# A list scheduler gets other prices and priorities, and plans the norm's affine part behind the norm's tail

## The chip, the cores and the metric

The kernel runs on one core of one Trainium2 chip. The metric is the time of one execution on the device in microseconds (us), the median of several runs. A core has five engines that the program uses, each with its own fixed list of instructions: TensorE (PE, with PEld for its weight loads), VectorE (DVE), ScalarE (ACT), GpSimd (POOL) and SyncE (SP, which here only starts transfers). An instruction waits for the one before it on its engine, and for semaphores of other engines where it needs their results.

## What is computed

Two layers of an encoder trunk on x of 256 tokens by 1024 channels, in float32:

```python
for l in range(DEPTH):                       # DEPTH = 2
    h = hybrid_mixer(x, ...)                 # three mixers on x, gated and merged, then @ w_out
    x = layer_norm(DEEPNORM_ALPHA * x + h, ln1_g[l], ln1_b[l])
    f = conv_glu_ffn(x, ...)                 # (silu(conv(x @ w_gate)) * (x @ w_up)) @ w_down
    x = layer_norm(DEEPNORM_ALPHA * x + f, ln2_g[l], ln2_b[l])

def layer_norm(x, g, b):
    mu = mean(x); var = mean((x - mu) ** 2)
    return (x - mu) * rsqrt(var + LN_EPS) * g + b
```

The three mixers are a differential attention, a gated delta rule in both directions (its chunks need a triangular solve) and a windowed attention. So there are four norms: two in layer 0 and two in layer 1. The first three feed the next stage, and the last one writes the output.

## The kernel before

**Weights and products.** Nearly all of the time goes into products of x with weight blocks of 128x1024 floats, each streamed from memory once (`raw_take`, three buffers) in a fixed order. To reach float32 accuracy at the fast rate, a block is split into a high part (`hi_take`, a rounding copy on ACT) and a low part (`lo_take`, a subtraction on DVE), and x likewise into `xTh` and `xTl` (x is held with channels on the partitions for this). `mm3` then issues three matmuls for each product: high by high, low by high, high by low. A projection block (`mm_proj_ch`) is 8 x 3 = 24 matmuls of 256 columns. Some products are made with tokens on the partitions instead (`mm_token_major`, 512 columns); `mm_run` and `ch_run` are those of the output projections `wo` and `fd`, from `proj_tok`.

**The mixers' solve.** The triangular solve goes over seven levels. At each level matmuls (`ch_solve`) are followed by merges on DVE (COPY_PREDICATED into `h_solve`), each of which the next level's matmuls need. Four such chains run at once. Projection matmuls, weight splits, attention steps and convolution steps fill the gaps.

**The norm.** `proj_tok` makes the first token half complete, then calls `norm.tail(0)`, then runs the matmuls that were kept for the second half (the last go into `ch_run`), then calls `norm.tail(1)`. `part` adds the product to x and takes the statistics. `tail` aggregates them on DVE, adds epsilon, takes the power -1/2 on POOL (`s_tail<-s_tail,nhalf`, the pow), normalizes on DVE (`q_tail`, four instructions), transposes on PE (`ch_tail`, `at_tail`), scales on ACT or DVE (`e_tail`) and splits the result into `xTh` (a copy on ACT or a CAST on DVE) and `xTl` (a subtraction on DVE). Only `xTh` and `xTl` go on to the next products. `finish` makes the same normalized value in the other layout, for the residual sum much later: the affine part, eight POOL instructions for each of the first three norms, four `x<-q_tail,ya_ln_params` (times g) and four `x<-x,ya_ln_params` (plus b).

**What sets the order.** The kernel's code records its operations in a `Plan`. Each record gets a price (`_cost`), its data dependences, and a rank: the longest priced path to the end, plus `op.urgent`, plus an entry of the table `PRIO` for its label. `schedule` then plays a greedy list scheduler over the five engines: it takes the instruction that can start earliest by its prices and, where several can, that of the highest rank. Copies, scalings and affine steps recorded through `A` can go to ACT or DVE, and the scheduler picks one. It also doubles a matmul's price when the window before it was thin. At the end the operations are issued in the order of their planned starts, and this fixes each engine's list. `plan.hold(i, j)` makes the planner start i no sooner than j; it acts in the plan alone:

```python
    def hold(self, i, j):

        self.ops[i].known.add(j)
```

Semaphores are set from data dependences when the operations are issued. All instructions are issued from one line, which is why the profile shows L191 everywhere; after the change it is L194. Tile names tell what an instruction is.

Of the kernel before, what the change touches and what calls it, by code (L numbers as in the profile page):

```python
# [10 lines left out]
F32 = mybir.dt.float32  # L11
F32R = mybir.dt.float32r
# [3 lines left out]
ALU = mybir.AluOpType  # L16
# [3 lines left out]
P = 128  # L20
# [28 lines left out]
PRIO = {(1, 'a', 0): 2.3, (0, 'ckv', 0): -3.3, (0, 'gz', 8): 4.3, (1, 'wb', 7): -1.6, (0, 'k', 'ab', 0): 1.4, (1, 'cq', 0): 2.7, (0, 'gz', 9): -1.8, (1, 'k', 'q', 1): 8.1, (0, 'gz', 7): -2.0, (1, 'solve'): -4.6, (1, 'c', 'cq', 0): 2.5, (1, 'k', 'k', 1): -2.8, (0, 'aq', 1): -5.9, (0, 'gz', 3): 3.5, (0, 'ab', 0): -7.3, (0, 'gz', 10): 1.9, (0, 'c', 'ckv', 0): 1.8, (0, 'c', 0): -2.1, (0, 'k', 'gate', 1): 0.2, (0, 'q', 0): -7.1, (0, 'a', 2): 3.4, (1, 'v', 0): -4.1, (1, 'gz', 7): -1.0, (1, 'a', 'aq', 0): 4.5, (0, 'k', 0): -6.2, (0, 'q', 1): -7.6, (0, 'solve'): -2.7, (1, 'aq', 1): -4.7, (1, 'a', 'aq', 1): -1.4, (0, 'wb', 1): -0.6, (1, 'q', 1): 5.3, (0, 'gate', 0): 7.8, (0, 'a', 0): -0.7, (0, 'wb', 7): -1.0, (1, 'k', 'v', 0): -6.5, (1, 'wb', 2): 3.6, (0, 'a', 3): 2.0, (1, 'c', 0): 3.5, (1, 'k', 'v', 1): -5.3, (0, 'k', 'v', 1): -8.6, (1, 'c', 3): 3.4, (1, 'gate', 1): 5.4, (1, 'scan'): -1.6, (1, 'a', 2): 6.9, (1, 'av', 0): 5.6, (1, 'wb', 9): 2.5, (1, 'gz', 6): 1.6, (0, 'gz', 0): 1.3}  # L49
LOADS = (11, 12, 12)  # L50
PIECES = 2
PAIRS = ("s", "yc")
# [7 lines left out]
           "ACT": {"PE": 0.27, "ACT": 0.14, "DVE": 0.14, "POOL": 0.18, "SP": 1.42},  # L60
           "DVE": {"PE": 0.26, "ACT": 0.2, "DVE": 0.13, "POOL": 0.18, "SP": 1.22},
           "POOL": {"PE": 0.2, "ACT": 0.15, "DVE": 0.1, "POOL": 0.11, "SP": 0.2}}
DMA_ISSUE = 1.2
TICK = 10.24 / 3
FULL = 3060
ENGINES = ("PE", "ACT", "DVE", "POOL", "SP")
# [62 lines left out]


class _Op:
    __slots__ = ("eng", "call", "cost", "deps", "known", "outs", "lat", "tiles", "new", "rank", "table", "start", "end", "urgent", "ways", "succ", "left", "ready", "group", "banks", "load", "columns", "label")


class Plan:
# [43 lines left out]
    def record(self, *ways):  # L179
        op = _Op()  # L180
        op.ways = []
        for eng, name, fn, args, kw in ways:
            aps = [v for v in list(args) + list(kw.values()) if isinstance(v, bass.AP)]
            outs = [kw["out"] if "out" in kw else args[0]]
# [4 lines left out]
            ins = [ap for ap in aps if not any(ap is o for o in outs)]  # L189
            table = TABLES.get(next((v for v in args if isinstance(v, AF)), None)) if name == "activation" else None  # L190
            op.ways.append((eng, lambda fn=fn, args=args, kw=kw: fn(*args, **kw), _cost(eng, name, outs, ins, args, kw), table))  # L191
# [42 lines left out]
    def emit(self):  # L234
# [51 lines left out]
    def schedule(self, users, order):  # L286
# [13 lines left out]
        for i, op in enumerate(ops):  # L300
            if op.left == 0:
                for way in op.ways:
                    pending[way[0]].append(i)
        table, done, begun = None, 0, 0.0

        shared = {}

        def available(op, eng):
# [9 lines left out]
            for tag, names in need.items():  # L318
                k = queue[tag]
                if len(slots[tag]) < len(names) or not (self.tags[tag][1] or set(order[tag][k:k + len(names)]) == set(names)):  # L320
                    return None
                t = max(t, sorted(slots[tag])[len(names) - 1] + (DMA_ISSUE if op.eng == "SP" else 0.0))
            return t

        while done < len(ops):
            best, other = None, {}
            for e, todo in pending.items():
# [23 lines left out]
            s, e, i = best  # L351
            op = ops[i]
# [29 lines left out]
            for j in op.succ:  # L382
                n = ops[j]
# [98 lines left out]
def tile_encoder_trunk(ctx: ExitStack, tc: tile.TileContext, a: dict, out: bass.AP, depth=DEPTH, tap=None):  # L482
    nc = tc.nc
    plan = Plan()
# [3 lines left out]
    V, S, G, TE, SY = [plan.engine(*e) for e in (("DVE", nc.vector), ("ACT", nc.scalar), ("POOL", nc.gpsimd), ("PE", nc.tensor), ("SP", nc.sync))]  # L488
# [147 lines left out]
    ready = {}  # L636
# [98 lines left out]
    class Norm:  # L735
# [11 lines left out]
        def tail(self, tt):  # L747
# [11 lines left out]
            for c in range(2):  # L759
                xs = x[:, tt, c * 512:(c + 1) * 512]  # L760
# [4 lines left out]
                for q in range(2):  # L765
# [280 lines left out]
    def gdn(l, pr, ys):  # L1046
# [444 lines left out]
```

## Time and profile before

| | |
|---|---|
| median of 3 runs | 1016.73 us |
| the runs | 1016.73, 1015.3, 1017.36 us |
| the profiled execution | 1016.1 us |
| its span in the trace | 1014.4 us |
| PE busy | 977.3 us (96%), 7598 matmuls |
| DVE busy | 744.0 us (73%) |
| ACT busy | 578.1 us (57%) |
| POOL busy | 113.6 us (11%) |
| read from memory | 163.12 MB, 162 GB/s over the span |

The busy share is an average over stages. A row of the timeline gives the start, the length, the engine, the instruction with its tiles and shape, and how many equal ones in a row it stands for; in brackets is the idle time before it and what ended it. Matmuls are pipelined, so a matmul's shown length is longer than the step from one to the next.

### The profile page before, as it was taken

The page shows a single profiled execution, that of the slowest core. Times are in us where ns is not written, and L with a number is a line of the kernel's source. Part 1 is how long each engine was busy: PE and PEld are TensorE (multiplying, and loading weights), DVE is VectorE, ACT ScalarE, POOL GpSimd, SP SyncE. Part 2 cuts the span into 40 slices and gives each one's busy share as a digit, 9 for nine tenths or more (in the row PEclk, how much of TensorE's full clock was granted, in tenths as well). Part 3 has the DMA queues.
Part 4 walks back from the last instruction along what each step waited for, and adds up shares of the span by engine and source line. Part 5 has one row for each costly group of instructions (what it writes and reads, how often), then busy time and mean ns, then how long its engine had stood idle before and what let it go on. Part 6 is the DMA issues. An engine that isn't in the chain of part 4 may idle for free. (4 is left out here: it accounts for less than half of the span.)

```text
span 1014.4 us, 19166 instructions
## 1 busy us (share of the span) xinstructions
PE 977.3 (96%) x7598; PEld 909.8 (90%) x7598; DVE 744.0 (73%) x1324; ACT 578.1 (57%) x1026; POOL 113.6 (11%) x108
## 2 busy tenths in 40 slices
PE   7998999999998999999989999999999989999996
PEld 5897899998986999998869989999999779999885
DVE  6789886775589777665679998875657878667555
ACT  5665864785355565553535776766644536555432
POOL 0510002100005100000144200001000150000000
PEclk9999999999999999999999999999999999999998
DMA  7552434464573765665625444334546746555661
GB/s 233 188 169 82 127 100 146 162 202 121 184 219 114 225 205 185 184 186 185 211 84 162 146 133 141 93 112 128 178 136 198 231 145 201 181 188 184 192 192 67
DMA packets 50109, 165.43 MB, mean 163 GB/s; under 512 B 5751, under 2 KB 11271, under 8 KB 50020
## 3 DMA queue, kind: packets, MB, share of 16 engines
q1 hardware_dynamic: 48644, 159.78, 49.7%
q0 software_dynamic: 1376, 4.43, 1.6%
q8 instruction: 59, 0.97, 0.4%
q14 instruction: 30, 0.25, 0.1%
HBM read 163.12 MB, written 1.07 MB: 162 GB/s over the span
## 5 line engine op out<-in xcount | busy, mean ns | idle before, releaser
L191 PE MATMUL mm_proj_ch<-xTh,lo_take 128*128 128x256 f32 x1488 | 420.1, 285 | 2.2 <-DVE lo_take L191 2.2
L191 PE MATMUL mm_proj_ch<-xTh,hi_take 128*128 128x256 f32 x1488 | 420.1, 285 | 0.9 <-ACT hi_take L191 0.9
L191 PE MATMUL mm_proj_ch<-xTl,hi_take 128*128 128x256 f32 x1488 | 418.1, 284 | 2.0 <-DVE xTl L191 2.0
L191 DVE TENSOR_TENSOR lo_take<-raw_take,hi_take 128x1024 fp32r<-128x1024 f32 x219 | 271.3, 1244 | 117.2 <-ACT hi_take L191 106.4
L191 ACT ACTIVATE hi_take<-raw_take 128x1024 fp32r<-128x1024 f32 x213 | 225.5, 1059 | 226.4 <-PE mm_proj_ch L191 143.4
L191 PEld LDWEIGHTS mm_proj_ch<-xTh,lo_take 128*128 128x128 f32 x1488 | 279.7, 189 | 5.5 <-DVE lo_take L191 4.1
L191 PEld LDWEIGHTS mm_proj_ch<-xTl,hi_take 128*128 128x128 f32 x1488 | 279.2, 189 | 5.7 <-DVE xTl L191 3.4
L191 PEld LDWEIGHTS mm_proj_ch<-xTh,hi_take 128*128 128x128 f32 x1488 | 279.7, 189 | 2.6 <-ACT hi_take L191 1.6
L191 DVE TENSOR_TENSOR lo_proj_tok<-raw_proj_tok,hi_proj_tok 128x1024 fp32r<-128x1024 f32 x50 | 61.2, 1225 | 49.2 <-ACT hi_proj_tok L191 49.0
L191 ACT ACTIVATE hi_proj_tok<-raw_proj_tok 128x1024 fp32r<-128x1024 f32 x50 | 53.1, 1061 | 74.1 <-PE mm_run L191 33.8
L191 POOL TENSOR_TENSOR s_tail<-s_tail,nhalf 128x1 f32<-128x1 f32 x8 | 6.8, 855 | 367.8 <-DVE s_tail L191 367.8
L191 DVE SCALAR_TENSOR_TENSOR z_conv_silu<-mm_proj_ch,col_params,z_conv_silu 128x254 f32<-128x254 f32 (+1 forms) x96 | 39.6, 473 | 0.5 <-ACT z_conv_silu L191 0.4
L191 ACT ACTIVATE e_window<-e_window,s_window 128x256 f32<-128x256 f32 x57 | 27.2, 498 | 7.3 <-DVE s_window L191 7.2
L191 POOL DMA_DIRECT2D ya_ln_params<-in_lnp_dram x16 | 8.8, 554 | 188.3 <-PE mm_product L191 96.6
L191 DVE SCALAR_TENSOR_TENSOR g_product<-g_product,mm_product 128x512 f32<-128x512 f32 x24 | 16.3, 683 | 16.3 <-PE mm_product L191 16.2
L191 PE MATMUL mm_run<-hi_proj_tok,ile_encoder_trunk 128*128 128x512 f32 x88 | 27.3, 389 | 0.0
L191 PE MATMUL mm_run<-hi_proj_tok,tile_encoder_trunk 128*128 128x512 f32 x88 | 27.3, 389 | 0.0
L191 ACT ACTIVATE e_attention<-e_attention,s_attention 128x256 f32<-128x256 f32 x48 | 23.3, 500 | 5.6 <-DVE s_attention L191 5.6
L191 PEld LDWEIGHTS <-h_solve 128*128 128x128 f16 x448 | 20.7, 99 | 5.6 <-issue 2.8
L191 PE MATMUL mm_product<-yc_window,hi_take 128*128 128x256 f32 x128 | 24.0, 284 | 1.1 <-DVE yc_window L191 0.6
L191 PE MATMUL mm_product<-ya_attention,hi_take 128*128 128x256 f32 x128 | 24.4, 286 | 0.0
L191 POOL TENSOR_TENSOR x<-q_tail,ya_ln_params 128x512 f32<-128x512 f32 x12 | 22.2, 1865 | 11.2 <-DVE q_tail L191 11.2
(344 smaller groups left out, 1714.9 us busy)
## 6 DMA issues: line engine op xcount, KB each, us to landing
raw_take<-in_w_dram SPq DMA_DIRECT2D x226, 512.0 KB, 3.7
raw_proj_tok<-in_w_dram SPq DMA_DIRECT2D x60, 512.0 KB, 3.6
G_load_G<-band SPq DMA_DIRECT2D x24, 192.0 KB, 3.5
ya_ln_params<-in_lnp_dram POOLq DMA_DIRECT2D x16, 256.0 KB, 6.2
x<-in_xT_dram SPq DMA_DIRECT2D x4, 256.0 KB, 4.2
x<-in_x_dram SPq DMA_DIRECT2D x2, 512.0 KB, 4.5
out_dram<-x SPq DMA_DIRECT2D x8, 128.0 KB, 1.8
_tile_encoder_trunk<-in_w_dram SPq DMA_DIRECT2D x4, 128.0 KB, 3.7
```

The lines of the kernel that those rows point to most:

```text
L191: op.ways.append((eng, lambda fn=fn, args=args, kw=kw: fn(*args, **kw), _cost(eng, name, outs, ins, args, kw), table))
```

## The change

The prices: a transfer's issue on SP goes from 0.1 us and its bytes to at least 0.45 us and on POOL from 1.04 to 0.55, its latency from 0.91 to 2.0 (SP) and from 3.0 to 3.5 (POOL), and matmul and pow prices get other formulas. The scheduler gets a model of DVE and POOL working at the same time (`beside`): a DVE instruction that has all its operands in SBUF and at least 64 columns takes up to twice its price while POOL works, and a POOL instruction up to 1.6 times. The table PRIO is replaced (48 entries before, 111 after). And the first of each pair of affine instructions is held behind the last operation of the norm's tail. What is computed stays the same, and so does the order of the weight stream.

```diff
-PRIO = {(1, 'a', 0): 2.3, (0, 'ckv', 0): -3.3, (0, 'gz', 8): 4.3,
+PRIO = {(0, 'a', 'ak', 0): 1.0, (0, 'a', 'ak', 1): 2.4, (0, 'a', 'aq', 0): -1.7,
...
-DMA_ISSUE = 1.2
+DMA_ISSUE = 0.3
...
-        return 1.04 if eng == "POOL" else max(0.1, math.prod(c for _, c in outs[0].ap) * 4 / 3.6e5)
+        return 0.55 if eng == "POOL" else max(0.45, math.prod(c for _, c in outs[0].ap) * 4 / 3.9e5)
...
-        wide = outs[0].dtype == F32 and ins[0].dtype == F32
-        n = _columns(outs[0])
-        slow = 4 if wide and name != "transpose" or ins[0].dtype == F32R and n < 256 else 2 if wide else 1
-        return max(n * slow / 2400, 0.025) + 0.0023
+        n, w = _columns(outs[0]), _columns(ins[0])
+        if ins[0].dtype == F32R and n >= 256:
+            return max(n * 17 / 16 / 2400, 0.119 if w == P else 0.113)
+        if ins[0].dtype in (F32, F32R):
+            passes = 1 if name == "transpose" else 2
+            return passes * max(n * 2 / 2400 + 0.0023, 0.112) * (1.35 if w < P and n > P else 1)
+        return max(n / 2400, 0.025) + 0.0023
...
-            return 0.3 + 0.165 * n
+            return 0.65 + 0.13 * n
...
-        op.lat = (3.0 if eng == "POOL" else 0.91) if name == "dma_start" else None
+        op.lat = (3.5 if eng == "POOL" else 2.0) if name == "dma_start" else None
...
+        op.sbuf = all(ap.space == bass.MemoryType.SB for ap in outs[:1] + ins) and _columns(outs[0]) >= 64
...
+        beside = {"DVE": 0.0, "POOL": 0.0}
...
+            if e == "DVE" and op.sbuf:
+                cost += min(cost, max(0.0, beside["POOL"] - s))
+                beside[e] = s + cost
+            elif e == "POOL" and not op.lat:
+                cost += 0.6 * min(cost, max(0.0, beside["DVE"] - s))
+                beside[e] = s + cost
...
             plan.urgent = 0.0
+            self.end = len(plan.ops) - 1
             if not self.last:
...
-                        G.tensor_tensor(xs, self.xh[tt][c], self.gb[c], op=ALU.mult)
+                        plan.hold(G.tensor_tensor(xs, self.xh[tt][c], self.gb[c], op=ALU.mult), self.end)
                         G.tensor_tensor(xs, xs, self.gb[2 + c], op=ALU.add)
```

What this does to the engines' lists is shown at three places. First POOL at the first norm of layer 1 (`s_tail_5` and `s_tail_6` are the pows of the first and the second token half, `q_tail_9` and `q_tail_10` the first half's normalized values, `q_tail_11` and `q_tail_12` the second's). Before:

```order
L191 TENSOR_TENSOR s_tail_5_1659<-s_tail_5_1658,nhalf 128x1
L191 TENSOR_TENSOR x<-q_tail_9_1660,ya_ln_params_9_1618 128x512
L191 TENSOR_TENSOR x<-q_tail_10_1663,ya_ln_params_10_1619 128x512
L191 TENSOR_TENSOR x<-x,ya_ln_params_11_1620 128x512
L191 TENSOR_TENSOR x<-x,ya_ln_params_12_1621 128x512
L191 TENSOR_TENSOR s_tail_6_1669<-s_tail_6_1668,nhalf 128x1
L191 TENSOR_TENSOR x<-q_tail_11_1670,ya_ln_params_9_1618 128x512
```

And after, with the waits that each instruction has:

```order
L194 TENSOR_TENSOR s_tail_5_1659<-s_tail_5_1658,nhalf 128x1 [waits DVE_49]
L194 TENSOR_TENSOR s_tail_6_1669<-s_tail_6_1668,nhalf 128x1 [waits DVE_49]
L194 TENSOR_TENSOR x<-q_tail_9_1660,ya_ln_params_9_1618 128x512 [waits DMASW2_49]
L194 TENSOR_TENSOR x<-q_tail_10_1663,ya_ln_params_10_1619 128x512 [waits DMASW3_49]
L194 TENSOR_TENSOR x<-q_tail_11_1670,ya_ln_params_9_1618 128x512 [waits DVE_49]
```

The second pow now stands ahead of all eight affine instructions, in this norm and in the other two. The first affine instruction waits only for the transfer of its parameters.

Second, DVE in the same norm, from the second half's sum to its first q_tail. Before:

```order
L191 SCALAR_TENSOR_TENSOR x<-x,ch_run_6_1666 128x512
L191 BN_STATS s___init__739_6_1623<-x 128x6 x2
L191 BN_AGGR s_tail_6_1667<-s___init__739_6_1623 128x2
L191 TENSOR_SCALAR s_tail_6_1668<-s_tail_6_1667 128x1
L191 TENSOR_TENSOR xTl<-e_tail_10_1665,xTh 128x2x128
L191 TENSOR_SCALAR q_tail_11_1670<-x,s_tail_6_1667,s_tail_6_1669 128x256
L191 TENSOR_SCALAR q_tail_12_1673<-x,s_tail_6_1667,s_tail_6_1669 128x256
```

And after:

```order
L194 SCALAR_TENSOR_TENSOR x<-x,ch_run_6_1666 128x512
L194 BN_STATS s___init__751_6_1623<-x 128x6 x2
L194 BN_AGGR s_tail_6_1667<-s___init__751_6_1623 128x2
L194 TENSOR_SCALAR s_tail_6_1668<-s_tail_6_1667 128x1
L194 TENSOR_TENSOR xTl<-e_tail_10_1665,xTh 128x2x128
L194 TENSOR_TENSOR lo_take_180_1701<-raw_take_187_1699,hi_take_180_1700 128x1024
L194 TENSOR_SCALAR q_tail_11_1670<-x,s_tail_6_1667,s_tail_6_1669 128x256
L194 TENSOR_SCALAR q_tail_12_1673<-x,s_tail_6_1667,s_tail_6_1669 128x256
```

The split of a weight block, which stood behind the whole tail, now stands where DVE waits for the pow; the other two norms have the same. On PE all 24 token matmuls of the first group (`mm_token_major_3`, `_5`, `_7`) now stand ahead of the second half's last transposes, and only two of the next group ahead of the first projection block.

Third, DVE in the solve of layer 0, from a third-level merge to a fourth-level one (`h_solve` with `ch_solve_9` and `ch_solve_15`). Before:

```order
L191 COPY_PREDICATED h_solve_3_214<-masks,ch_solve_9_230 128x128x4
L191 COPY_PREDICATED h_solve_2_213<-masks,ch_solve_8_229 128x128x4
L191 ISA e_attention_1_323,s_attention_1_320<-at_attention_1_322,G_load_G_1_319 128x256
L191 ISA s_attention_1_320 128x1
L191 COPY_PREDICATED h_solve_6_218<-masks,ch_solve_12_233 128x128x4
L191 COPY_PREDICATED h_solve_5_217<-masks,ch_solve_11_232 128x128x4
L191 TENSOR_TENSOR yc_attention_3_313<-mm_proj_ch_9_304,yc_attention_1_311 64x512 x2
L191 TENSOR_TENSOR yc_attention_4_314<-mm_proj_ch_9_304,yc_attention_2_312 64x512 x2
L191 COPY_PREDICATED h_solve_3_214<-masks,ch_solve_15_236 128x64x8
```

And after:

```order
L194 COPY_PREDICATED h_solve_3_214<-masks,ch_solve_9_230 128x128x4
L194 SCALAR_TENSOR_TENSOR z_conv_silu_4_295<-mm_proj_ch_8_288,col_params_1_93,z_conv_silu_4_295 128x254
L194 TENSOR_TENSOR q_stacked_4_287<-mm_proj_ch_7_279,q_stacked_4_287 64x512
L194 COPY_PREDICATED h_solve_6_218<-masks,ch_solve_12_233 128x128x4
L194 COPY_PREDICATED h_solve_2_213<-masks,ch_solve_8_229 128x128x4
L194 SCALAR_TENSOR_TENSOR z_conv_silu_4_295<-j_conv_silu_4_296,z_conv_silu_4_295 128x512
L194 TENSOR_TENSOR lo_take_23_390<-raw_take_23_388,hi_take_23_389 128x1024
L194 COPY_PREDICATED h_solve_5_217<-masks,ch_solve_11_232 128x128x4
```

Convolution steps, a query step and a weight split now stand among the merges, and the attention steps come later. From the solve's first merge to the sixth level's, DVE has three lo_takes more in layer 0 and PE eight projection matmuls more; in layer 1 PE has 18 projection matmuls fewer there and DVE as many lo_takes as before. Over the whole kernel 15 instructions go from ACT to DVE, and the rest only changes places.

More of the change, by code (lines that the diff above doesn't have):

```diff
@@ L48 @@
 WHOLE = ()
-PRIO = {(1, 'a', 0): 2.3, (0, 'ckv', 0): -3.3, (0, 'gz', 8): 4.3, (1, 'wb', 7): -1.6, (0, 'k', 'ab', 0): 1.4, (1, 'cq', 0): 2.7, (0, 'gz', 9): -1.8, (1, 'k', 'q', 1): 8.1, (0, 'gz', 7): -2.0, (1, 'solve'): -4.6, (1, 'c', 'cq', 0): 2.5, (1, 'k', 'k', 1): -2.8, (0, 'aq', 1): -5.9, (0, 'gz', 3): 3.5, (0, 'ab', 0): -7.3, (0, 'gz', 10): 1.9, (0, 'c', 'ckv', 0): 1.8, (0, 'c', 0): -2.1, (0, 'k', 'gate', 1): 0.2, (0, 'q', 0): -7.1, (0, 'a', 2): 3.4, (1, 'v', 0): -4.1, (1, 'gz', 7): -1.0, (1, 'a', 'aq', 0): 4.5, (0, 'k', 0): -6.2, (0, 'q', 1): -7.6, (0, 'solve'): -2.7, (1, 'aq', 1): -4.7, (1, 'a', 'aq', 1): -1.4, (0, 'wb', 1): -0.6, (1, 'q', 1): 5.3, (0, 'gate', 0): 7.8, (0, 'a', 0): -0.7, (0, 'wb', 7): -1.0, (1, 'k', 'v', 0): -6.5, (1, 'wb', 2): 3.6, (0, 'a', 3): 2.0, (1, 'c', 0): 3.5, (1, 'k', 'v', 1): -5.3, (0, 'k', 'v', 1): -8.6, (1, 'c', 3): 3.4, (1, 'gate', 1): 5.4, (1, 'scan'): -1.6, (1, 'a', 2): 6.9, (1, 'av', 0): 5.6, (1, 'wb', 9): 2.5, (1, 'gz', 6): 1.6, (0, 'gz', 0): 1.3}
+PRIO = {(0, 'a', 'ak', 0): 1.0, (0, 'a', 'ak', 1): 2.4, (0, 'a', 'aq', 0): -1.7, (0, 'a', 'aq', 1): 4.1, (0, 'a', 0): 4.8, (0, 'a', 2): -0.9, (0, 'a', 3): 1.2, (0, 'ab', 0): -2.2, (0, 'ak', 0): -0.5, (0, 'aq', 0): -2.5, (0, 'av', 0): 13.8, (0, 'c', 'cq', 0): 7.3, (0, 'c', 0): -3.1, (0, 'c', 2): -3.9, (0, 'c', 3): -3.4, (0, 'ckv', 0): -1.5, (0, 'cq', 0): 5.4, (0, 'cq', 1): -0.9, (0, 'gate', 0): -11.1, (0, 'gate', 1): -4.8, (0, 'gz', 0): 2.1, (0, 'gz', 1): 5.1, (0, 'gz', 2): -13.4, (0, 'gz', 3): -0.7, (0, 'gz', 4): 0.8, (0, 'gz', 5): -4.0, (0, 'gz', 6): 1.9, (0, 'gz', 7): 6.8, (0, 'gz', 8): 4.5, (0, 'gz', 9): 4.8, (0, 'k', 'ab', 0): 3.8, (0, 'k', 'gate', 0): -3.0, (0, 'k', 'gate', 1): -12.8, (0, 'k', 'k', 0): 4.0, (0, 'k', 'k', 1): -3.4, (0, 'k', 'q', 0): 13.4, (0, 'k', 'q', 1): 4.1, (0, 'k', 'v', 0): -2.6, (0, 'k', 'v', 1): 2.5, (0, 'k', 1): 0.7, (0, 'q', 0): 7.7, (0, 'q', 1): 2.7, (0, 'scan'): -1.5, (0, 'v', 0): 3.3, (0, 'v', 1): 4.3, (0, 'wb', 11): -4.3, (0, 'wb', 2): -4.5, (0, 'wb', 3): -2.4, (0, 'wb', 4): 12.2, (0, 'wb', 5): 15.1, (0, 'wb', 6): 1.5, (0, 'wb', 7): 1.5, (0, 'wb', 8): 3.0, (0, 'wb', 9): 5.1, (1, 'a', 'ak', 1): -2.7, (1, 'a', 'aq', 0): 2.7, (1, 'a', 'aq', 1): -3.6, (1, 'a', 1): 18.3, (1, 'a', 2): -1.4, (1, 'a', 3): 4.5, (1, 'ab', 0): -5.3, (1, 'ak', 0): -1.6, (1, 'ak', 1): -0.9, (1, 'aq', 1): 4.3, (1, 'av', 0): 1.0, (1, 'c', 'cq', 0): -5.9, (1, 'c', 'cq', 1): -0.7, (1, 'c', 0): 3.0, (1, 'c', 1): -4.1, (1, 'c', 3): 3.5, (1, 'ckv', 0): -7.5, (1, 'cq', 0): 4.3, (1, 'finish'): -7.0, (1, 'gate', 0): 0.8, (1, 'gate', 1): -5.8, (1, 'gz', 1): 0.8, (1, 'gz', 10): 0.6, (1, 'gz', 2): -0.2, (1, 'gz', 3): 8.3, (1, 'gz', 4): -10.6, (1, 'gz', 5): -5.0, (1, 'gz', 6): -4.4, (1, 'gz', 7): -2.2, (1, 'gz', 8): 2.2, (1, 'gz', 9): -3.5, (1, 'k', 'ab', 0): -1.8, (1, 'k', 'gate', 0): 6.4, (1, 'k', 'gate', 1): -1.2, (1, 'k', 'k', 1): -0.3, (1, 'k', 'q', 0): 1.3, (1, 'k', 'q', 1): -5.5, (1, 'k', 'v', 0): 0.5, (1, 'k', 'v', 1): -9.8, (1, 'k', 0): -3.1, (1, 'q', 0): -0.2, (1, 'q', 1): -7.1, (1, 'solve'): -5.8, (1, 'v', 0): -5.5, (1, 'v', 1): -2.2, (1, 'wb', 0): 2.9, (1, 'wb', 1): -1.5, (1, 'wb', 10): -8.6, (1, 'wb', 11): -6.4, (1, 'wb', 2): -7.2, (1, 'wb', 3): -5.8, (1, 'wb', 4): -3.4, (1, 'wb', 5): -2.9, (1, 'wb', 6): 0.7, (1, 'wb', 7): -3.3, (1, 'wb', 8): -0.5, (1, 'wb', 9): 4.9}
@@ L131 @@
 class _Op:
-    __slots__ = ("eng", "call", "cost", "deps", "known", "outs", "lat", "tiles", "new", "rank", "table", "start", "end", "urgent", "ways", "succ", "left", "ready", "group", "banks", "load", "columns", "label")
+    __slots__ = ("eng", "call", "cost", "deps", "known", "outs", "lat", "tiles", "new", "rank", "table", "start", "end", "urgent", "ways", "succ", "left", "ready", "group", "banks", "load", "columns", "label", "sbuf")
 class Plan:
```

## The prediction

> **What bounds the kernel now.** I read the page first, then the windows, then the waits of PE, last the timelines of DVE and POOL around the three norms that the change touches.
>
> ```profile
> span 1014.4 us, 19166 instructions
> PE 977.3 (96%) x7598; PEld 909.8 (90%) x7598; DVE 744.0 (73%) x1324; ACT 578.1 (57%) x1026; POOL 113.6 (11%) x108
> 854.57 91.14 PE mm_proj_ch L191 x768
> ```
>
> PE is the bound: 977.3 of 1014.4 us. In the third row (the chain that ended last: start, length, count) a projection matmul takes 91.14/768 = 0.119 us, and nothing in this change alters that work. So the time moves only with what PE loses. Here are its waits at the three norms and one in the layer-0 solve (start, length, instruction, in brackets the idle time before and its releaser):
>
> ```profile
> 318.50 0.78 PE L191 MATMUL mm_token_major<-g_weights,xTl 128*128 128x512 f32 x1 [2.04 <-DVE xTl L191]
> 326.67 0.51 PE L191 MATMUL mm_proj_ch<-xTl,hi_take 128*128 128x256 f32 x2 [1.51 <-DVE xTl L191]
> 510.98 0.50 PE L191 MATMUL mm_token_major<-hi_take,xTl 128*128 128x512 f32 x1 [0.58 <-DVE xTl L191]
> 515.46 0.44 PE L191 MATMUL ch_tail<-tri,q_tail 128*128 128x128 f32 x2 [2.10 <-DVE q_tail L191]
> 818.98 0.44 PE L191 MATMUL ch_tail<-tri,q_tail 128*128 128x128 f32 x2 [2.13 <-DVE q_tail L191]
> 827.72 0.39 PE L191 MATMUL mm_proj_ch<-xTh,lo_take 128*128 128x256 f32 x1 [0.38 <-DVE lo_take L191]
> 78.88 0.39 PE L191 MATMUL mm_proj_ch<-xTh,lo_take 128*128 128x256 f32 x1 [1.24 <-DVE lo_take L191]
> ```
>
> After each long wait a window follows at half clock (columns: window, length, busy us and count of PE, PEld, DVE, ACT, POOL, granted clock, DMA share, GB/s); four longer windows of the mixers stand below:
>
> ```profile
> 318.55:321.96 3.41, 3.41 (x8) 2.64 (x9) 3.19 (x10) 0.07 (x1) 0.67 (x1) 0.50 0.47 156
> 516.53:519.94 3.41, 3.37 (x11) 2.26 (x9) 3.41 (x5) 1.02 (x3) 3.41 (x3) 0.50 0.00 0
> 820.31:823.72 3.41, 3.41 (x13) 2.78 (x12) 3.41 (x6) 1.08 (x3) 3.18 (x4) 0.50 0.02 5
> 75.00:100.00 25.00, 21.79 (x275) 19.66 (x273) 24.09 (x48) 13.80 (x21) 1.32 (x3) 0.93 0.23 69
> 100.00:125.00 25.00, 23.73 (x280) 22.49 (x276) 20.85 (x49) 21.73 (x50) 0.00 (x0) 1.00 0.46 143
> 581.00:606.00 25.00, 24.06 (x313) 22.36 (x312) 24.81 (x47) 19.05 (x35) 0.61 (x2) 1.00 0.37 115
> 625.00:650.00 25.00, 23.52 (x257) 22.44 (x256) 21.76 (x55) 20.94 (x51) 0.70 (x1) 1.00 0.38 120
> ```
>
> A window of 3.41 us at clock 0.50 does 1.7 us less work. So the three norms cost PE 2.04+1.51+1.7 = 5.25, 0.58+2.10+1.7 = 4.4 and 2.13+0.38+1.7 = 4.2: 13.9 us in all. The Trainium skill (TensorE: Matmul & The Clock Gate, Part 1) lets the clock fall only after a window of about 3.4 us that is idle. By that rule these half clocks would not hang on waits of 2 us, and 5.1 of the 13.9 would stay whatever the norms do; the dearest gain below would then be 6 and not 11.
>
> **The norms: what the wait is worth.** What PE waits for is the second half's tail. It can begin when the last ch_run matmul is done; call that moment E. The rows: last ch_run of PE, DVE's first use of it, first q_tail, last xTl.
>
> ```profile
> 313.04 1.56 PE L191 MATMUL ch_run<-x_weights,kk_product 128*128 128x512 f32 x6
> 318.37 0.68 DVE L191 SCALAR_TENSOR_TENSOR x<-x,ch_run 128x512 f32<-128x512 f32 x1
> 321.11 1.06 DVE L191 TENSOR_SCALAR q_tail<-x,s_tail,s_tail 128x256 f32<-128x256 f32 x3
> 327.18 1.53 DVE L191 TENSOR_TENSOR xTl<-e_tail,xTh 128x256 fp32r<-128x256 f32 x3
> 506.66 1.87 PE L191 MATMUL ch_run<-g_weights,tile_encoder_trunk 128*128 128x512 f32 x7
> 512.27 0.68 DVE L191 SCALAR_TENSOR_TENSOR x<-x,ch_run 128x512 f32<-128x512 f32 x1
> 514.99 1.39 DVE L191 TENSOR_SCALAR q_tail<-x,s_tail,s_tail 128x256 f32<-128x256 f32 x4 [0.45 <-POOL s_tail L191]
> 521.79 1.08 DVE L191 TENSOR_TENSOR xTl<-e_tail,xTh 128x256 fp32r<-128x256 f32 x3
> 811.50 1.63 PE L191 MATMUL ch_run<-x_weights,kk_product 128*128 128x512 f32 x6
> 814.07 0.67 DVE L191 SCALAR_TENSOR_TENSOR x<-x,ch_run 128x512 f32<-128x512 f32 x1
> 818.51 1.06 DVE L191 TENSOR_SCALAR q_tail<-x,s_tail,s_tail 128x256 f32<-128x256 f32 x3 [1.68 <-POOL s_tail L191]
> 825.45 1.08 DVE L191 TENSOR_TENSOR xTl<-e_tail,xTh 128x256 fp32r<-128x256 f32 x3
> ```
>
> E is 314.60, 508.53 and 813.13; DVE comes 3.8, 3.7 and 0.9 us later, held up by first-half work that ran beside the affine part. The last xTl ends 14.1, 14.3 and 13.4 us after E. From first q_tail to last xTl it takes 7.6, 7.9 and 8.0 us.
>
> With the change, POOL does the second pow ahead of all affine work, so the first half's tail is free of it and DVE can take up E at once (0.3 taken for the handover). From x<-x,ch_run to q_tail lie 514.99-512.27 = 2.7 us, with 0.45 idle; the order now puts a lo_take into that idle time, which adds its own length less 0.45.
>
> ```profile
> L191 DVE TENSOR_TENSOR lo_take<-raw_take,hi_take 128x1024 fp32r<-128x1024 f32 x219 | 271.3, 1244 | 117.2 <-ACT hi_take L191 106.4
> 817.92 0.55 POOL L191 TENSOR_TENSOR s_tail<-s_tail,nhalf 128x1 f32<-128x1 f32 x1
> 809.65 5.65 POOL L191 TENSOR_TENSOR x<-q_tail,ya_ln_params 128x512 f32<-128x512 f32 x2 [3.51 <-DVE q_tail L191]
> 811.88 0.28 DVE L191 CAST xTh<-e_tail 128x256 fp32r<-128x256 f32 x1
> 812.76 1.38 DVE L191 CAST xTh<-e_tail 128x256 fp32r<-128x256 f32 x1
> 820.13 0.96 DVE L191 TENSOR_SCALAR q_tail<-x,s_tail,s_tail 128x256 f32<-128x256 f32 x1
> 821.01 1.58 DVE L191 CAST xTh<-e_tail 128x256 fp32r<-128x256 f32 x2
> 823.15 0.86 DVE L191 TENSOR_TENSOR xTl<-e_tail,xTh 128x256 fp32r<-128x256 f32 x1
> 823.94 1.59 DVE L191 CAST xTh<-e_tail 128x256 fp32r<-128x256 f32 x2
> ```
>
> So q_tail starts at E + 0.3 + 2.7 + 0.8 = E + 3.8 (before: 6.5, 6.5, 5.4). That is a gain of 2.7, 2.7 and 1.6 us.
>
> **What takes it back.** The hold exists in the plan alone. It is not a data dependence, and in the order the first affine instruction has no wait on DVE left: it follows the second pow on POOL at once, some ten microseconds ahead of the tail's last instruction. All eight affine instructions then run beside the second half's tail, where four did before. What four cost there is in the rows: a q_tail of 0.96 for 0.35 (1.06/3), CAST pairs of 1.58 and 1.59 for 0.56, an xTl of 0.86 for 0.36 (1.08/3): 0.6+1.0+1.0+0.5 = 3.1, so 0.8 for each affine instruction. Four more cost 3.2. The bounds for one are 0, if DVE keeps POOL out (811.88: a CAST at 0.28 while POOL's first affine instruction was pending), and 1.1 each (812.76: 1.38 for 0.28), 8.8 for eight. I take 0.8, since it is the mean of this very stretch.
>
> The Trainium skill (SBUF — State Buffer, Who interferes with whom) calls the port pair that DVE and GpSimd share an exclusive lock that blocks the loser for a whole instruction, with issue order deciding who loses. The rows have both outcomes. By that rule at its worst, eight DVE instructions would each wait out an affine instruction, which is the second half of rival C.
>
> The last xTl then ends at E + 3.8 + 7.6..8.0 + 3.2, about 15.0 us after E, and up to 0.3 more where CASTs have moved to DVE; before it was 13.4 to 14.3. What PE has to do meanwhile: 24 token matmuls, at the pace of these rows (15 matmuls from the first to the last),
>
> ```profile
> 812.96 0.64 PE L191 MATMUL mm_token_major<-g_weights,xTh 128*128 128x512 f32 x2
> 816.46 0.39 PE L191 MATMUL mm_token_major<-yc_weights,xTh 128*128 128x512 f32 x1
> ```
>
> 0.233 each, 5.6 us; two of the next token group, 0.5; the first projection block, 24 x 0.119 = 2.85: 9.0 with nothing for the transposes. Before, a dozen token matmuls of the second half filled in here; now they stand later. So PE loses 15.0 + 0.4 - 9.0 = 6.4 us per norm, 19.2 in all against 13.9: +5.3. Transposes left out of the work make this some tenths too large for each norm: I take **+4.5**. Bounds: with nothing from the affine part the last xTl comes at E + 8.5 and PE loses next to nothing, but the affine part then lies on the weight splits (1 us a norm, estimated from 0.8 on the first split or two that PE waits for), so -13.9+3 = -11; with 1.1 for each of eight, 2.4 worse a norm than my sum, +12.
>
> **The mixers.** Prices and priorities move other work. In the layer-0 solve 78.88 waits 1.24 for a lo_take, and the window 75 to 100 has clock 0.93 (1.7 us). In the new order a few projection matmuls more stand ahead of the solve, so I count half of these 2.9 as gained: -1.5. Between the first and the sixth merge of that solve DVE gets three more lo_takes (3 x 1.24 = 3.7) and PE eight more projection matmuls (8 x 0.119 = 1.0); the other pieces that come and go nearly balance. DVE had 0.9 of 25 free in the window 75 to 100, and 4.15 in the next, so about 1.2 of the remaining 2.7 shows: -0.3 for layer 0. In the layer-1 solve PE loses 18 projection matmuls beside an equally busy DVE (24.81 of 25): +2.1, given back where they stand now, as far as there are holes (1.48 in 625 to 650, and 1.27 in 100 to 125 of the other layer): net +0.5 to +1. Weight stream and its order are the same. Everything together: **0**, with bounds of -8 (all idle time of 75 to 125, 3.2+1.3, the half clock 1.7 and the 1.5 of 625 to 650) and +8 (2.7+2.1, and a half clock in two windows, 3.4). The 15 instructions that go from ACT to DVE lie in these sums.
>
> **Sum.** The profiled execution took 1016.1 us (span 1014.4 and 1.7 around it), 0.6 below the median of 1016.7. 1016.1 + 4.5 + 0 = 1020.6, so 1021 for the median.
>
> **Rivals.**
> *A, faster:* POOL is kept off the port through the tail. For it: 809.65, where two affine instructions took 5.65 us while DVE went through a run of short work at its own pace. It decides at one point: whether DVE goes from the lo_take through four q_tails into the CASTs without a gap. Against it: the e_tails wait for PE's transposes, and in all three norms CASTs after an e_tail were blocked. Price -11: 1006. A half success would be 1012.
> *B, faster:* the norms as I say, but the mixers' holes close (-8): 1013. For it: the prices now rest on measured durations. Against: DVE is already full in both solves.
> *C, slower still:* the solves starve PE (+4.5 and +8), or every affine instruction blocks fully (+12): 1029, and 1025 at half of it. For it: DVE at 24.81 of 25 in the layer-1 solve, where it gets no less work.
> *D, the change does nothing:* the stretch E to xTl comes out at 14 as before, lo_take and added contention balancing the earlier start: 1016 to 1017. It is the low edge of my own sum.
>
> Chances: forecast 0.40 (its own range 1018 to 1025), A 0.22, B 0.10, C 0.15, D 0.13. About 2 us (0.2%) is what a measurement of this kernel can tell. A, B give faster 0.32; D and a little of the forecast give same 0.17; the rest is slower, 0.51. Range 1006 to 1028: it leaves out the far ends of A and C.
>
> **What would show it.** Right: in the new profile POOL's first affine instruction starts within 0.3 us of the second pow's end; CAST and xTl of the second half take over 1 us beside it up to the last one; x<-x,ch_run follows E within 1 us; PE's waits move from ch_tail to mm_proj_ch<-xTh or xTl of the first projection block, 5 us or more a norm. Wrong: the last xTl ends by E + 10, affine instructions stretch to 3 us and lie on lo_takes (A), or the three norms lose about the same 14 us and the difference lies in 75 to 125 or 575 to 650 (B, C).

## The result and the profile after

The change made the kernel slower: 1032.1 us median of 4 runs (1030.5 to 1034.0) against 1016.8 (1015.3 to 1017.4), a ratio of 1.0154 (95% interval 1.0133 to 1.0174). The direction of the forecast was right, and its size was not: 1021 was forecast, and 1032 lies outside its range. The profiled execution of the changed kernel took 1031.8 us, with this page:

```profile
span 1030.1 us, 19146 instructions
PE 984.5 (96%) x7598; PEld 916.1 (89%) x7598; DVE 749.6 (73%) x1339; ACT 569.7 (55%) x1011; POOL 105.9 (10%) x108
```

The busy shares hardly move, so they don't tell where 15.7 us of span come from. The ends of the three ch_run groups (E, as in the prediction) and the end of the last matmul cut the span into four parts, with the second half of one norm at the start of each of the last three. These rows of PE give the ends in the changed kernel:

```profile
314.22 1.40 PE L194 MATMUL ch_run<-x_weights,kk_product 128*128 128x512 f32 x5
511.83 1.31 PE L194 MATMUL ch_run<-g_weights,tile_encoder_trunk 128*128 128x512 f32 x5
823.05 1.56 PE L194 MATMUL ch_run<-x_weights,kk_product 128*128 128x512 f32 x6
1018.00 2.88 PE L194 MATMUL ch_run<-g_weights,ile_encoder_trunk 128*128 128x512 f32 x12
```

| part (us) | before | after | difference |
|---|---|---|---|
| start to E of layer 0's first norm | 314.6 | 315.6 | +1.0 |
| from there (that norm, FFN) to the next E | 193.9 | 197.5 | +3.6 |
| from there (second norm, layer 1's mixers) to the next E | 304.6 | 311.5 | +6.9 |
| from there (layer 1's first norm, FFN) to the last matmul | 192.5 | 196.3 | +3.8 |

All three parts with a norm lose, and the one that also has mixers loses most. The parts, here and below, come from one execution of each kernel. The first part has the same lists of PE, DVE and ACT in the kernel before and in three others below (hold_only, before_real_hold, before_no_affine), and took 313.5 to 315.0 us there, so a difference of a part under about 1.5 us tells nothing by itself. The norm of layer 1 in the changed kernel, first POOL, then DVE from the second half's statistics on (start, length, instruction, count):

```profile
826.68 0.67 POOL L194 TENSOR_TENSOR s_tail<-s_tail,nhalf 128x1 f32<-128x1 f32 x1 [9.23 <-DVE s_tail L194]
827.33 3.19 POOL L194 TENSOR_TENSOR x<-q_tail,ya_ln_params 128x512 f32<-128x512 f32 x2
831.07 2.66 POOL L194 TENSOR_TENSOR x<-q_tail,ya_ln_params 128x512 f32<-128x512 f32 x2 [0.55 <-DVE q_tail L194]
833.69 5.42 POOL L194 TENSOR_TENSOR x<-x,ya_ln_params 128x512 f32<-128x512 f32 x4
```

```profile
826.85 1.22 DVE L194 TENSOR_TENSOR lo_take<-raw_take,hi_take 128x1024 fp32r<-128x1024 f32 x1
827.99 3.32 DVE L194 TENSOR_SCALAR q_tail<-x,s_tail,s_tail 128x256 f32<-128x256 f32 x4
831.87 2.01 DVE L194 CAST xTh<-e_tail 128x256 fp32r<-128x256 f32 x2
834.45 0.84 DVE L194 TENSOR_TENSOR xTl<-e_tail,xTh 128x256 fp32r<-128x256 f32 x1
835.21 1.36 DVE L194 CAST xTh<-e_tail 128x256 fp32r<-128x256 f32 x1
836.49 3.23 DVE L194 TENSOR_TENSOR xTl<-e_tail,xTh 128x256 fp32r<-128x256 f32 x3
```

The affine part starts at 827.33, as the pow ends, and its eight instructions run to 839.1. The tail's last xTl ends at 839.7: the affine part lies over the whole second half of the tail that it was to wait for. What PE waits for there, and at the worst places of the other two norms:

```profile
326.47 0.58 PE L194 MATMUL mm_proj_ch<-xTl,hi_take 128*128 128x256 f32 x1 [1.59 <-DVE xTl L194]
330.44 0.58 PE L194 MATMUL mm_proj_ch<-xTl,hi_take 128*128 128x256 f32 x1 [1.89 <-DVE xTl L194]
523.87 0.39 PE L194 MATMUL mm_proj_ch<-xTl,hi_take 128*128 128x256 f32 x1 [1.78 <-DVE xTl L194]
527.97 0.58 PE L194 MATMUL mm_proj_ch<-xTl,hi_take 128*128 128x256 f32 x1 [1.80 <-DVE xTl L194]
830.72 0.44 PE L194 MATMUL at_tail<-tri,q_tail 128*128 128x128 f32 x2 [0.78 <-DVE q_tail L194]
835.34 0.39 PE L194 MATMUL mm_proj_ch<-xTl,hi_take 128*128 128x256 f32 x1 [1.55 <-DVE xTl L194]
836.63 0.39 PE L194 MATMUL mm_proj_ch<-xTh,hi_take 128*128 128x256 f32 x1 [0.42 <-DVE xTh L194]
839.44 0.58 PE L194 MATMUL mm_proj_ch<-xTl,hi_take 128*128 128x256 f32 x1 [2.08 <-DVE xTl L194]
```

And the granted clock around these waits (columns as in the prediction: the window before, then the whole stretch at half clock):

```profile
322.74:326.15 3.41, 1.63 (x9) 1.02 (x9) 3.41 (x6) 1.56 (x4) 3.18 (x4) 1.00 0.01 2
326.15:336.39 10.24, 8.03 (x33) 7.41 (x34) 8.17 (x9) 1.06 (x1) 3.95 (x3) 0.50 0.28 92
520.71:524.12 3.41, 1.33 (x7) 0.69 (x7) 3.41 (x6) 1.36 (x4) 3.41 (x4) 1.00 0.01 2
524.12:530.95 6.83, 4.98 (x22) 4.16 (x22) 4.13 (x4) 0.00 (x0) 3.51 (x3) 0.50 0.00 0
834.74:838.15 3.41, 1.60 (x8) 1.07 (x8) 3.41 (x4) 0.00 (x0) 3.41 (x4) 1.00 0.00 0
838.15:844.98 6.83, 5.54 (x26) 5.54 (x27) 4.47 (x5) 1.06 (x1) 3.10 (x5) 0.50 0.58 172
```

Half clock now lasts three windows, two and two, where it was one each. The last wait of each norm falls into that stretch, so that a further window is thin. A stretch at half clock loses half of PE's busy time in it: 4.0 + 2.5 + 2.8 = 9.3 us, against 5.1 before. With the waits (4.8, 4.9 and 5.3 us with the small ones), the norms lose 24.2 us from E to 35 us behind it. Counted in the same way, small waits too, the kernel before loses 15.0 (the 13.9 of the prediction are its long waits and the half clock). So the norms lose 9.2 us more than before.

### The profile page after: what moved, and what is told of

Same layout as the page of the kernel before. It is cut to its first block, busy times and chain, and to the rows that moved or that the text cites. A ratio compares the mean times of both kernels' runs of the same rounds, so it can differ in the third digit from the quotient of the medians.

```text
span 1030.1 us, 19146 instructions
## 1 busy us (share of the span) xinstructions
PE 984.5 (96%) x7598; PEld 916.1 (89%) x7598; DVE 749.6 (73%) x1339; ACT 569.7 (55%) x1011; POOL 105.9 (10%) x108
## 3 DMA queue, kind: packets, MB, share of 16 engines
HBM read 163.12 MB, written 1.07 MB: 159 GB/s over the span
## 5 line engine op out<-in xcount | busy, mean ns | idle before, releaser
L194 PE MATMUL mm_proj_ch<-xTl,hi_take 128*128 128x256 f32 x1488 | 422.9, 287 | 10.7 <-DVE xTl L194 10.7
L194 ACT ACTIVATE hi_take<-raw_take 128x1024 fp32r<-128x1024 f32 x212 | 222.4, 1058 | 227.7 <-PE mm_proj_ch L194 167.4
L194 PEld LDWEIGHTS mm_proj_ch<-xTl,hi_take 128*128 128x128 f32 x1488 | 283.0, 191 | 14.1 <-DVE xTl L194 12.9
L194 PEld LDWEIGHTS mm_proj_ch<-xTh,hi_take 128*128 128x128 f32 x1488 | 282.7, 191 | 7.4 <-issue 2.0
L194 PE MATMUL mm_product<-ya_gdn,hi_take 128*128 128x256 f32 x128 | 23.4, 283 | 0.0
```

## The experiments

Theory 1: the affine part, which on the chip runs beside the tail that PE waits for, is what the norms lose; the new lists lose some 5 us more in the mixers. Theory 2: the new lists of DVE and PE are the loss, wherever the affine part runs. The table gives the median, the ratio to the kernel before on the same chip with its interval, and the four parts of the span. The kernels ran on several chips, where the kernel before took 1016.5 to 1017.8 us; where two chips differ enough to matter, both reckonings are given.

| kernel | us | ratio | four parts |
|---|---|---|---|
| before + hold in the plan (hold_only) | 1021.3 | 1.0042 [1.0029, 1.0056] | 315.0, 196.7, 305.4, 194.4 |
| change + real hold (real_hold) | 1013.1 | 0.9956 [0.9942, 0.9970] | 315.6, 189.4, 307.4, 188.7 |
| change, no affine part (no_affine) | 1008.6 | 0.9922 [0.9898, 0.9946] | 314.6, 188.8, 305.0, 188.5 |
| change without the hold (no_hold) | 1036.7 | 1.0194 [1.0157, 1.0231] | 318.2, 196.6, 314.5, 198.5 |
| change, POOL's list of before (old_pool) | 1026.2 | 1.0076 [1.0060, 1.0092] | 316.1, 196.2, 309.5, 194.4 |
| before + real hold (before_real_hold) | 1005.2 | 0.9871 [0.9853, 0.9889] | 314.9, 190.2, 302.1, 188.1 |
| change + real hold, old table (rh_old_prio) | 1024.1 | 1.0063 [1.0046, 1.0080] | 317.0, 195.2, 308.2, 192.3 |
| before + real hold, new table (rh_new_prio) | 1016.0 | 0.9983 [0.9969, 0.9996] | 318.7, 192.3, 306.1, 188.0 |
| before + real hold, matmul prices (add_pe) | 1026.0 | 1.0086 [1.0055, 1.0117] | 311.3, 194.4, 314.0, 191.2 |
| before + real hold, transfer prices (add_dma) | 1005.9 | 0.9893 [0.9873, 0.9914] | 307.4, 196.1, 301.5, 188.0 |
| before + real hold, beside and pow (add_beside) | 1011.4 | 0.9948 [0.9930, 0.9967] | 313.9, 193.2, 303.8, 191.9 |
| before, no affine part (before_no_affine) | 999.5 | 0.9822 [0.9805, 0.9840] | 313.5, 189.2, 299.5, 187.7 |

**The hold alone.** Into the kernel before:

```diff
+            self.end = len(plan.ops) - 1
...
-                        G.tensor_tensor(xs, self.xh[tt][c], self.gb[c], op=ALU.mult)
+                        plan.hold(G.tensor_tensor(xs, self.xh[tt][c], self.gb[c], op=ALU.mult), self.end)
```

> The kernel before with one edit, the hold in the plan; PE, DVE, ACT and SP have the lists of before, and POOL alone is reordered: the second pow ahead of all eight affine instructions. Theory 1 (the affine part now runs beside the second half's tail, which PE waits for, and that is what costs): the first half gets free as it does with the whole change, and the second half pays; last xTl at about E + 14.5 in all three norms, half clock there longer than one window, 1020 to 1028 us. Theory 2 (the new lists of DVE and PE cost it, such as the weight split ahead of q_tail and the lost fillers, and where the affine part runs is worth nothing): 1013 to 1017 us, since only the wait of the second pow goes away.

It took 1021.3 us, 4 more than before, with POOL's list as the only difference (the other engines' instructions have the order of before in the traces). POOL and DVE at the norm of layer 1:

```profile
819.79 2.55 POOL L191 TENSOR_TENSOR x<-q_tail,ya_ln_params 128x512 f32<-128x512 f32 x2
825.66 5.32 POOL L191 TENSOR_TENSOR x<-x,ya_ln_params 128x512 f32<-128x512 f32 x4
```

```profile
819.85 2.96 DVE L191 TENSOR_SCALAR q_tail<-x,s_tail,s_tail 128x256 f32<-128x256 f32 x3 [0.46 <-POOL s_tail L191]
829.78 2.15 DVE L191 TENSOR_TENSOR xTl<-e_tail,xTh 128x256 fp32r<-128x256 f32 x3
```

Three q_tails take 2.96 us here, 1.06 before. E is 817.05, so the last xTl ends at E + 14.9, against E + 13.4 before, although q_tail starts at E + 2.8 in place of 5.4. So an order that starts the tail earlier ends it later. One thing came otherwise than expected: half clock lasted one window in each norm, as before, and not longer. Theory 2 allowed no loss here and falls as the only cause.

**The hold made real.** Into the change, with all its other lists as they are; it differs from the change by three POOL instructions that carry the data dependence:

```diff
+    behind = cp.tile([P, 1], F32, name="behind")
...
                         plan.hold(G.tensor_tensor(xs, self.xh[tt][c], self.gb[c], op=ALU.mult), self.end)
+                        if tt == c == 0:
+                            plan.first[len(plan.ops) - 1] = lambda: nc.gpsimd.tensor_tensor(behind, xTl[:, KD - 1, T - 1:T].bitcast(F32), nhalf[:, 0:1], op=ALU.mult)
...
+            if i in self.first:
+                self.first[i]()
             ops[i].call()
```

> The whole change, with the hold made real: a POOL instruction of one column that reads the tail's last xTl stands ahead of each norm's affine part, all other lists being those of the change. Theory 1: the affine part leaves the second half's tail, the last xTl comes at E + 9 to 10, the three norms lose 1 to 3 us each in place of 8, and the time falls to 1008 to 1016 us; the affine part then lies on the weight splits, which costs up to 1 us a norm. Theory 2: 1028 to 1033 us, as for the change.

1013.1 us: 19 less than the change. The last xTl ends 9.0 to 9.2 us after E in the three norms. DVE goes through the same list as in the changed kernel's rows above, now alone:

```profile
815.75 1.38 DVE L195 TENSOR_SCALAR q_tail<-x,s_tail,s_tail 128x256 f32<-128x256 f32 x4
818.61 0.48 DVE L195 CAST xTh<-e_tail 128x256 fp32r<-128x256 f32 x2
819.72 0.41 DVE L195 TENSOR_TENSOR xTl<-e_tail,xTh 128x256 fp32r<-128x256 f32 x1
820.05 0.29 DVE L195 CAST xTh<-e_tail 128x256 fp32r<-128x256 f32 x1
820.25 1.09 DVE L195 TENSOR_TENSOR xTl<-e_tail,xTh 128x256 fp32r<-128x256 f32 x3
```

Row by row the affine part had cost 1.94, 1.53, 0.43, 1.07 and 2.14 us: 7.1 for eight instructions, 0.89 each. The granted clock stays at 1.00 through the norm, and PE is busy for nearly all of it:

```profile
812.00:837.00 25.00, 24.66 (x178) 22.73 (x177) 21.13 (x37) 13.21 (x19) 16.24 (x10) 1.00 0.48 160
```

**The affine part left out of the change.** The same two lines are planned and then not issued.

> The whole change with the 24 affine instructions left out (the residual sums then use the wrong x); all other lists are those of the change. It is the floor of what the affine part costs anywhere. Theory 1: as with the hold made real, or up to 3 us less: 1006 to 1014 us. Theory 2: 1027 to 1032 us.

1008.6 us. So of the 23.5 us that the affine part costs in the change, the real hold gives back 19, and 4.5 stay where the held part lies on weight splits.

**The change without the hold.** The one line of the hold goes back to that of before.

> The whole change without the hold: new prices, new priorities and the new model of DVE and POOL, with the first half's affine instructions ahead of the second pow again. Theory 1: the norms cost about what they cost before, and only the mixers' part of the loss stays (about 4 us): 1018 to 1023 us. Theory 2: 1029 to 1033 us, the lists of PE and DVE being nearly those of the change.

1036.7 us: above the ranges of both theories. The planner makes other lists when the hold goes, on every engine, so this is not the change with one thing less. All four parts lose against before (+3.6, +2.7, +9.9, +6.0). It speaks for Theory 2 as a second cause, and the next kernel was made to take the two apart.

**POOL's list alone set back in the change.** After the plan is made, the first half's four affine instructions get a place just ahead of the second pow:

```diff
+        for n, (i, pw) in enumerate(self.early):
+            ops[i].start = ops[pw].start - 1e-3 + (ops[i].start - ops[pw].start) * 1e-6
         for op in sorted(ops, key=lambda o: o.start):
             op.call()
```

> The whole change with only POOL's list set back: the first half's four affine instructions stand ahead of the second pow again, and PE, DVE, ACT and SP keep the lists of the change. Theory 1: the affine part is spread over both halves as before, the norms lose 18 to 23 us in place of 28, 1022 to 1027 us. Theory 2 (the new lists of DVE and PE make the norms slow, which the slow run without the hold speaks for): 1031 to 1037 us.

1026.2 us. The lists themselves cost 8 us where the affine part is spread as before (1026.2 against 1017.8 on that chip), and the change costs 15 on its own chip, so with the lists of the change POOL's new order costs 7 us (6 by the medians alone); with those of before it cost 4. So each theory has its share: about 7 us are POOL's order, and about 8 the lists. In waits and half clock the three norms lose 17.5 us here, against 24.2 in the change and 15.0 before: at the norms the lists cost 2.5 us, and most of their 8 lies elsewhere.

This kernel and the one without the hold also show how much a plan can move by itself. Both have the first half's four affine instructions ahead of the second pow, on POOL only the order among these four differs, and prices and table are the same; yet the lists that the planner made without the hold cost 10 us more (1036.7 against 1026.2).

**The real hold in the kernel before.** Both edits above, without prices and table.

> The kernel before with the hold made real: PE, DVE, ACT and SP keep the lists of before, and POOL does each norm's affine part behind a one-column instruction that reads the tail's last xTl. Theory 1 (the affine part beside a tail is the loss at the norms, and the new lists lose some 5 us more in the mixers): the norms gain as in the change with a real hold, the mixers stay as before, 1003 to 1008 us. Theory 2 (the new lists are worth something themselves, and the real hold needs them): 1012 to 1017 us.

1005.2 us, 1.3% faster than the kernel before and, with add_dma below (1005.9 on another chip, not to be told apart), the fastest of all that compute everything. The lists of the change cost 8 us here too (1013.1). The norm of layer 1:

```profile
807.18 0.69 DVE L192 SCALAR_TENSOR_TENSOR x<-x,ch_run 128x512 f32<-128x512 f32 x1
809.92 1.06 DVE L192 TENSOR_SCALAR q_tail<-x,s_tail,s_tail 128x256 f32<-128x256 f32 x3 [0.45 <-POOL s_tail L192]
814.00 1.09 DVE L192 TENSOR_TENSOR xTl<-e_tail,xTh 128x256 fp32r<-128x256 f32 x3
815.01 4.58 DVE L192 TENSOR_TENSOR lo_take<-raw_take,hi_take 128x1024 fp32r<-128x1024 f32 x3
```

```profile
805.00:830.00 25.00, 25.00 (x170) 22.87 (x169) 22.14 (x40) 13.68 (x22) 15.50 (x10) 1.00 0.46 151
500.00:525.00 25.00, 25.00 (x150) 21.21 (x148) 18.89 (x38) 12.80 (x25) 12.33 (x9) 1.00 0.36 116
```

E is 807.14, and the last xTl ends 8.0 us later. PE is never idle in the two windows. Three lo_takes take 4.58 us beside the held part.

**Prices or table.** With the real hold in both, the table and the prices were exchanged one at a time.

> The change with the hold made real and the table of priorities of before: new prices and the new model of DVE and POOL under the old table. If the new table is what costs the mixers some 5 us, 1004 to 1010 us; if the new prices cost it, or if the table fits only the prices that it was searched with, 1012 to 1025 us.

> The kernel before with the hold made real and only the new table of priorities, under the old prices. If the new table is what costs the mixers, 1010 to 1016 us, some 5 us above the kernel before with a real hold; if the prices cost it, 1003 to 1009 us; if table and prices belong together, 1015 us and more.

Old prices and old table 1005.2, new prices alone 1024.1, new table alone 1016.0, both 1013.1. So each costs alone, 19 and 11 us, and together 8: under the new prices the new table takes back 11 of their 19. Both fit the case in which table and prices belong together, the second only just: it is also the upper end of the case in which the table costs by itself. Of the 6.3 us between the profiled spans of real_hold and before_real_hold, 5.3 lie in the third part, which has layer 1's mixers.

**Which price.** Three kernels add one group of prices to before_real_hold, under the old table: the matmul formula; DMA_ISSUE with the bytes and latency of transfers; `beside` with the price of the pow.

> The kernel before with the hold made real (1005.2 us) and, under the old table of priorities, only the new matmul prices. All new prices together under the old table cost 19 us (1024.1). If the matmul prices are what costs it, 1015 to 1025 us; if not, 1003 to 1009 us. If no single price costs it but any new plan under an old table does, each of these three kernels takes 1009 to 1018 us.

> The same with only the new prices of transfers (issue, bytes and latency). If these cost it, through weight blocks that are planned late, 1015 to 1025 us; if not, 1003 to 1009 us; if any new plan under an old table costs, 1009 to 1018 us.

> The same with only the model of DVE and POOL working at the same time and the new price of the pow. If these cost it, 1015 to 1025 us; if not, 1003 to 1009 us; if any new plan under an old table costs, 1009 to 1018 us.

The matmul prices cost 21 us (1026.0, just above the range for it), beside with pow 6 (1011.4, in the range of any new plan), and the transfers nothing that can be told from the noise between chips (1005.9). That the transfers' total stays is a balance of parts: the first is 7.5 us shorter and the second 5.9 longer. The three costs add up to more than the 19 of all prices together, and each group was tried in one plan only. As a plan alone can move 10 us, that the matmul prices as such are what costs, and not this one plan, isn't shown. With the matmul prices, the third part goes from 302.1 to 314.0. These are PE's longest waits after the first at the kernel's start (total, count, longest), and two windows of layer 1's mixers:

```profile
PE ch_gdn_scalars L195 <- DVE gg_gdn_scalars L195: 3.3, 1, 3.3
PE ch_solve L195 <- ACT v_solve L195: 3.2, 5, 1.0
PE ch_solve L195 <- ACT h_solve L195: 2.3, 7, 0.5
```

```profile
575.00:600.00 25.00, 22.68 (x271) 20.95 (x270) 25.00 (x61) 17.89 (x34) 0.60 (x1) 1.00 0.35 116
600.00:625.00 25.00, 21.20 (x267) 19.16 (x267) 20.25 (x50) 19.97 (x51) 2.30 (x2) 1.00 0.25 73
```

With the old matmul prices the second window reads:

```profile
600.00:625.00 25.00, 24.40 (x247) 23.48 (x244) 21.64 (x52) 16.64 (x36) 1.74 (x1) 1.00 0.45 143
```

PE loses 3.2 us more there, and the transfers run at half the rate. DVE is not full in 600 to 625 (20.25), but it is full all through 575 to 600 (25.00). PE waits for chains of the solve and of the delta rule's scalars (`gdn_scalars`) that run through DVE and ACT; whether these lack DVE time or only stand too late in the lists isn't settled. The formula's 0.119 us for a projection matmul is what the trace has, while the old one gave 0.109; the truer price made the worse lists. Why, these runs don't show.

**The floor.** The kernel before with the affine part left out.

> The kernel before with the 24 affine instructions left out (the residual sums then use the wrong x), all other lists those of before. It is the floor for a hold: if the held affine part costs nearly nothing where it lies on the weight splits, 1003 to 1006 us, as with the real hold (1005.2); if it costs there what it cost in the change (1013.1 against 1008.6 with it left out), 999 to 1003 us.

999.5 us, in the dearer of the two cases. In the kernel before the affine part cost 17 us (1016.5 on that chip), and 5.7 stay after the real hold (4.4 if each is taken against the kernel before on its own chip), 1.5 to 1.9 for each norm.

## Why the prediction was right or wrong

*The hold acts in the plan alone:* right. The first affine instruction starts as the second pow ends in all three norms, and making the hold real takes 19 us off.

*E and the last xTl:* right. In the norm of layer 1 q_tail starts at 827.99, which is E + 3.4 (3.8 was forecast), and the last xTl ends at E + 15.1 (15.0); in the other two norms it is E + 15.4 and 15.1. The signs that were named for this came too: x<-x,ch_run follows E at once, and PE's waits move to the first projection block, though with 4.8 to 5.3 us a norm some stay below the 5 that were named.

*0.8 us for each affine instruction:* nearly right, 0.89. Neither rival A (POOL kept off the port) nor a full block of every instruction came about. POOL lost once in each norm, behind the lo_take (two affine instructions took 3.19 us), and from then on DVE's instructions on SBUF waited. The Trainium skill (SBUF — State Buffer, Who interferes with whom) has this lock and says that issue order decides who blocks. The trace agrees: of the four q_tails the first two took 1.40 and 1.36 us, each to just behind the end of an affine instruction (829.23 and 830.52), and the other two 0.40 each, while POOL itself waited for a q_tail.

*"So PE loses 15.0 + 0.4 - 9.0 = 6.4 us per norm":* this step failed, because it stops at the last xTl. Up to there (and the 0.4) it held: waits of 14.9 us and half clock of 3.2 make 18.2 in the three norms, and 19.2 were forecast. But half clock went on behind the last xTl and took another 6.0 us of PE's work (2.5, 1.2 and 2.4), for which the sum had nothing, although it had counted 5.1 for half clock before the change. There the one window of each norm lay ahead of the last xTl. So the norms lost 9.2 us more than before, not 4.5. By cause, 6.7 of the 9.2 go with POOL's order and 2.5 with the lists (old_pool). Neither gives the long half clock alone: with POOL's order alone (hold_only) it takes 4.9 us at the norms, with the lists alone (old_pool) 6.4, in the change 9.3. That the kernel got slower through POOL's order was no luck: that order costs 4 us under the old lists and 7 under the new.

*Half clock hangs on waits of about 2 us:* right, and it should have been carried on into the sum behind the last wait. Windows in which PE was busy for 1.33 to 1.63 of 3.41 us were followed by half clock in the change, and with the real hold there is none around the norms. The Trainium skill (TensorE: Matmul & The Clock Gate, Part 1) has the clock fall after an idle window; here half an idle one was enough in each of the three places, and the measurement decides.

*The mixers at 0:* the second step that failed, though it stayed within the bounds of -8 and +8. The new lists cost some 5 to 6 us outside the norms (in old_pool 8 less the 2.5 at the norms). In the change 4.4 us lie in the third part, with layer 1's mixers, beyond what its norm loses, where I had +0.5 to +1; the +1.0 of the first part is within the noise. With the real hold in both kernels the third part differs by 5.3. The terms of that step were single gaps (a lo_take more, 18 projection matmuls fewer). What costs in their place stays open: PE's idle time behind that norm grows by 2.4 us only, and no single wait there is over 0.5 us.

*The affine part on weight splits, 1 us a norm:* somewhat too small: 1.5 in the change (1013.1 - 1008.6 over three norms) and 1.5 to 1.9 in the kernel before.

*Range and chances:* slower was given 0.51. The two terms that were too small, by 4.7 us at the norms and by 5 to 6 outside them, make up the 11 us by which the forecast missed; that both erred the same way is what took the time out of the range. The range took the dear ends of rival C one at a time, and not together.

## What to carry to other kernels

A hold that acts in a planner alone is a wish: look in the built program for the wait, and if there is none, give the instruction a data dependence. When a wait is priced, price with it the clock that follows it; here half clock added 9.3 us to 14.9 us of waits. A table of priorities fits the prices that it is used with: exchanged one at a time, each cost more than both together. Truer prices aren't by themselves a better plan, and one plan is too few to judge a price by.

## What was not expected of the hardware

While DVE and POOL both have work on SBUF queued, they take turns, one instruction each: a q_tail went from 0.41 to 1.40 us, a CAST from 0.29 to 1.36, each ending just behind the affine instruction beside it. Instructions that read PSUM pass: the pairs of e_tail took 0.72 us beside POOL and 0.73 without it:

```profile
831.23 0.72 DVE L194 TENSOR_SCALAR e_tail<-at_tail,col_params 128x128 f32<-128x128 f32 x2
```

```profile
817.96 0.73 DVE L195 TENSOR_SCALAR e_tail<-at_tail,col_params 128x128 f32<-128x128 f32 x2 [0.83 <-PE at_tail L195]
```

And the one-column POOL instruction of the real hold took 2.24 us while two lo_takes ran (821.26 to 823.6):

```profile
821.43 2.24 POOL L819 TENSOR_TENSOR behind<-xTl,nhalf 128x1 f32<-128x1 f32 x1 [6.31 <-DVE xTl L195]
821.26 2.36 DVE L195 TENSOR_TENSOR lo_take<-raw_take,hi_take 128x1024 fp32r<-128x1024 f32 x2
```

How thin a window has to be for half clock can be read over all 14 traces, leaving out the first and last few windows of each. Of the windows at full clock, all 17 in which the profile shows PE busy for under 1.64 of the 3.41 us were followed by half clock, 10 of the 66 between 1.64 and 2.40 us, and none above. So a wait needn't fill a window, and PE's busy time alone doesn't give a sharp limit.
